# Scan over head pairs: four pairs in sequence against pairs that overlap, with the 32x32 inverses built from 16x16 blocks

## The chip, the cores and the metric

The kernel runs on one core of one Trainium2 chip. The metric is device time in microseconds (us), the median over runs of one program. TensorE is called PE, VectorE DVE, ScalarE ACT, GpSimd POOL; SP issues DMAs.

## The reference, cut to what matters

A two-layer backbone (512 latent and 256 context tokens, width 1024). Each layer mixes the tokens in four ways, merges them with gates and adds an expert network. The change touches the second mixer alone, RWKV-7 time mixing: for each of 8 heads a 64x64 state S runs once forward and once backward over the tokens, the context's state carried into the latent tokens.

```
def step(S, inp):
    r, w, k, v, kk, a = inp
    sa = jnp.einsum('bhij,bhj->bhi', S, kk)
    S = S * w[:, :, None, :] - sa[..., None] * (kk * a)[:, :, None, :] + v[..., None] * k[:, :, None, :]
    return S, jnp.einsum('bhij,bhj->bhi', S, r)
...
o = o_f + o_b
mu = jnp.mean(o, axis=-1, keepdims=True)
var = jnp.mean(jnp.square(o - mu), axis=-1, keepdims=True)
o = (o - mu) * lax.rsqrt(var + RWKV_GN_EPS) * ln_g + ln_b
y = (o + bonus).reshape(B, L, RWKV_W) * f['g']
```

## The kernel before

The scan is done in chunks of 64 tokens: 12 chunks, 4 of context and 8 latent. Heads go in pairs (two heads of 64 fill 128 rows), so a layer has four pairs, and `rwkv_pair` (L690) does one pair for both directions d. Its parts, in the order in which they stand:

- **Gram products** (L709): for each chunk a 128x128 product of the scaled keys BK and queries AR, four chunks and two heads to a group, each group masked out of PSUM by DVE into G (L712). Six groups in a pair.
- **Inverse.** Each chunk needs the inverse of a triangular 64x64 matrix. Its two diagonal 32x32 blocks are copied out of G (L718, ACT), transposed on DVE so that one block lies in one partition (L721, L722), and inverted there by `eliminate` (L735): row by row, a product of two SBUF tiles into `tmp` (L742) and a subtraction from X (L745), 52 of each in a pair, in two column strips that alternate. Transposes bring the result back (L756 to L761), and the off-diagonal block follows by two 32x32 products on PE (L764 to L777). The result is TT.
- **KV** (L732): products of G's first half with the values, copied to SBUF by ACT (L734).
- **Recurrence**, 12 steps (L829). One step: four products with the state S (L836), an addition w0s (DVE, L839), four products with TT (L844), two copies to UV (ACT L846, DVE L847), four products with `nat` (L857), and the new S (L868, DVE) out of PSUM and `sp`, the decayed old S from POOL (L867). One step late come the outputs (L807 and L809: the part from S and the part from G, in turn for each of four places) and their copies into Yn (L818, L820). `nat` is a transposed key chunk with a sign (L182, L792).
- **Finish**: the normalisation of Yn, transposes, bonus and gate (L877 to L903).

The finish of a pair is placed behind the next pair's elimination. A scheduler sets the order on each engine from the code's order and its own costs. It fills TensorE with `gate_lat` (L905): 32 chunks of 24 matmuls with 512 columns that project the latent gates. A chunk's weights are loaded by SP, rounded to wH by ACT (L204), and the remainder wL is made by POOL (L205); ACT takes the result out of PSUM (L911). Each weight tile has two buffers and so has the PSUM tile `pl` of a chunk. Attention (L1156 on) comes after the scan.

## Time and profile before

| | |
|---|---|
| Median of 3 runs | 6446.6 us (6434.26 to 6451.8) |
| The profiled execution's own time | 6431.72 us |
| Its span | 6429.8 us |
| Granted TensorE clock, mean | 0.942 of full |
| PE / DVE / ACT / POOL busy | 90% / 70% / 37% / 34% |

The span is the time from the first to the last instruction of the profiled execution. The scan of layer 0 lies at about 580 to 1110 us, that of layer 1 at about 4110 to 4612 us. A PE that is shown busy may still wait inside of its pipeline, so the prediction reads starts of instructions beside busy time. A float32 matmul stands in the trace as two records and a float32r matmul (the gates) as one.

### The profile page before, as it was taken

How to read it: one execution, taken by the hardware profiler on the slowest of the kernel's cores; microseconds unless marked ns; L12 is line 12 of the kernel's file. 1: busy time of each engine (PE TensorE's matmuls, PEld its weight loads, DVE VectorE, ACT ScalarE, POOL GpSimd, SP SyncE). 2: the span in 40 equal slices, each digit the busy share in tenths (PEclk: the TensorE clock that was granted, in tenths of full speed). 3: DMA queues.
4: the chain of work that ended last, by engine and by line, in shares of the span. 5: the costliest groups of instructions: out<-in, count | busy, mean ns of one | idle time of the engine just before them, and what ended most of it. 6: DMA issues, size and time to landing. Idle time of an engine off the chain costs nothing. (4 is left out here: it accounts for less than half of the span.)

```text
span 6429.8 us, 95669 instructions
## 1 busy us (share of the span) xinstructions
PE 5798.9 (90%) x35605; PEld 4788.5 (74%) x35605; DVE 4503.3 (70%) x9402; ACT 2367.3 (37%) x4585; POOL 2210.1 (34%) x1721
## 2 busy tenths in 40 slices
PE   8898998999898998889899788799899888999998
PEld 5677665678776876777677576666667878999998
DVE  6535555677698847888888774545567798588887
ACT  3223222444436842222222332122345467433333
POOL 1101222000138835566555211132200168444442
PEclk9899997999998999999999899889999999999999
DMA  4456222032435678888899535422221546888896
GB/s 173 160 191 192 81 84 79 18 100 69 137 118 198 237 267 309 307 310 315 315 335 329 184 108 179 132 90 77 77 65 55 157 162 229 298 295 291 295 333 245
DMA packets 532161, 1220.90 MB, mean 190 GB/s; under 512 B 46320, under 2 KB 249200, under 8 KB 524016
## 3 DMA queue, kind: packets, MB, share of 16 engines
q1 hardware_dynamic: 339728, 718.16, 34.1%
q0 software_dynamic: 111168, 406.63, 17.3%
q10 hardware_dynamic: 80800, 90.00, 4.1%
q8 instruction: 281, 4.60, 0.3%
q14 instruction: 184, 1.51, 0.1%
HBM read 1041.41 MB, written 173.21 MB: 189 GB/s over the span
## 5 line engine op out<-in xcount | busy, mean ns | idle before, releaser
L1545 PE MATMUL pu<-HX,wH 128*128 128x512 f32 (+2 forms) x4608 | 1325.5, 371 | 10.0 <-ACT ga L1784 5.6
L1545 PEld LDWEIGHTS pu<-HX,wH 128*128 128x128 f32 x4608 | 854.1, 194 | 114.0 <-ACT ga L1784 7.1
L1545 PE MATMUL pu<-HX,wL 128*128 128x512 f32 (+2 forms) x2304 | 846.8, 368 | 40.5 <-POOL wL L1533 35.8
L1008 POOL DMA_INDIRECT row<-in_peer_u,gix x384 | 489.3, 1274 | 510.0 <-DVE row L1655 275.6
L1008 POOL DMA_INDIRECT row<-in_peer_v,gix x384 | 494.2, 1287 | 450.3 <-DVE accn L1664 222.5
L1637 ACT CAST wH<-row 128x1024 fp32r<-128x1024 f32 x384 | 401.9, 1047 | 618.5 <-DMA row<-in_peer_v 282.3
L1796 PE MATMUL pa<-CL,wH 128*128 128x512 f32 (+1 forms) x1536 | 566.8, 369 | 23.7 <-DVE CL L1776 23.2
L1796 PE MATMUL pa<-CH,wH 128*128 128x512 f32 (+1 forms) x1536 | 564.2, 367 | 22.5 <-ACT CH L1771 22.4
L1655 DVE SCALAR_TENSOR_TENSOR row<-row,hn 128x1024 f32<-128x1024 f32 x384 | 502.1, 1318 | 95.7 <-DMA row<-in_peer_u,gix 94.6
L1653 DVE TENSOR_TENSOR wL<-row,wH 128x1024 fp32r<-128x1024 f32 x384 | 477.4, 1243 | 126.5 <-ACT wH L1637 126.5
L1796 PE MATMUL pa<-CH,wL 128*128 128x512 f32 (+1 forms) x1536 | 562.6, 366 | 0.0
L1664 DVE SCALAR_TENSOR_TENSOR accn<-row,gcw,accn 128x1024 f32<-128x1024 f32 x381 | 518.4, 1371 | 61.2 <-DMA row<-in_peer_v,gix 60.2
L1545 PEld LDWEIGHTS pu<-HX,wL 128*128 128x128 f32 x2304 | 444.3, 193 | 98.7 <-POOL wL L1533 41.7
L204 ACT CAST wH<-wr 128x1024 fp32r<-128x1024 f32 (+1 forms) x222 | 231.0, 1043 | 572.5 <-PE pl L176 182.2
L176 PE MATMUL pl<-X,wH 128*128 128x512 f32 x1024 | 398.9, 452 | 3.4 <-DVE qk L585 3.0
L205 POOL TENSOR_TENSOR wL<-wr,wH 128x1024 fp32r<-128x1024 f32 x64 | 215.0, 3364 | 542.3 <-ACT wH L204 491.9
L1456 POOL TENSOR_SCALAR B<-cst,T 128x128 f32<-128x128 f32 x330 | 381.6, 1164 | 34.3 <-PE pg L1472 21.6
L980 POOL TENSOR_TENSOR lnst<-lnst,mhalf 128x4 f32<-128x4 f32 (+3 forms) x8 | 9.4, 1180 | 1096.5 <-DVE lnst L979 1096.5
L1796 PEld LDWEIGHTS pa<-CL,wH 128*128 128x128 f32 x1536 | 291.6, 190 | 69.4 <-DVE CL L1776 38.3
L1796 PEld LDWEIGHTS pa<-CH,wH 128*128 128x128 f32 x1536 | 291.8, 190 | 62.3 <-ACT CH L1771 30.4
L205 DVE TENSOR_TENSOR wL<-wr,wH 128x1024 fp32r<-128x1024 f32 (+1 forms) x158 | 191.1, 1212 | 189.9 <-ACT wH L204 189.0
L1796 PEld LDWEIGHTS pa<-CH,wL 128*128 128x128 f32 x1536 | 291.8, 190 | 30.6
(400 smaller groups left out, 13244.3 us busy)
## 6 DMA issues: line engine op xcount, KB each, us to landing
row<-in_peer_v SPq DMA_DIRECT2D x256, 512.0 KB, 5.9
wr<-in_uT SPq DMA_DIRECT2D x128, 512.0 KB, 4.9
row<-in_uT SPq DMA_DIRECT2D x128, 512.0 KB, 5.7
wr<-in_ada_w SPq DMA_DIRECT2D x96, 512.0 KB, 6.6
wr<-in_w_gate SPq DMA_DIRECT2D x96, 512.0 KB, 3.7
gdr<-gall SPq DMA_DIRECT2D x32, 1024.0 KB, 6.4
Gt<-gdr SPq DMA_DIRECT2D x32, 1024.0 KB, 13.0
gdr<-big SPq DMA_DIRECT2D x24, 1024.0 KB, 4.8
```

The lines of the kernel that those rows point to most:

```text
L176: pe.matmul(o, lw, rw[:, lo:hi], start=(k == 0 and a == 0), stop=(k == nk - 1 and a == 2))
L204: ac.copy(H, raw)
L205: lsplit[0] = (split or ve).tensor_tensor(L, raw, H.bitcast(F32), op=OP.subtract)
L980: gp.tensor_tensor(st, st, mhalf.to_broadcast([P, 2 * nb]), op=OP.pow)
L1008: gp.indirect_dma_start(out=rows, out_offset=None, in_=tab, in_offset=bass.IndirectOffsetOnAxis(ap=ix, axis=0))
L1456: (gp if e == "gp" else ve).tensor_scalar(B[:, j, :], iota, T3[:, 1, t_ + j:t_ + j + 1], T3[:, 2, t_ + j:t_ + j + 1], op0=OP.is_equal, op1 ...
L1545: pe.matmul(pw[:, :hi - lo], w[:, k, :], x[:, k, :], start=(k == 0 and i == 0), stop=(k == DC - 1 and i == 2))
L1637: ac.copy(H, ready[nx[1]])
L1653: ve.tensor_tensor(L, raw, H.bitcast(F32), op=OP.subtract)
L1655: ve.scalar_tensor_tensor(raw, raw, 1.0, hn[y], op0=OP.mult, op1=OP.mult, accum_out=acts[y][:, j:j + 1])
L1664: ve.scalar_tensor_tensor(accn[y], raw, gcw[y][:, j:j + 1], accn[y], op0=OP.mult, op1=OP.add)
L1796: pe.matmul(pv[:, :TD], w[:, ds], x, start=(k == 0 and i == 0 and (fresh or s == 0)), stop=(k == 1 and i == 2 and (fresh or s == NS - 1)))
```

## The change

The pair's work is split into four generators: `gram` (Gram products and KV), `inverse`, `recurrence` and `finish`. `together` interleaves them: behind the steps of pair hp's recurrence stand the finish of pair hp-1, the inverse of pair hp+1 and the Gram products of pair hp+2. Operands are no longer loaded as half sequences but in pieces: four chunks for a Gram group, three for KV, one step (both directions) for the recurrence; that is 424 more DMAs on SP. G is split into GA (for KV and the inverse) and GR (for the outputs), each with its own mask instruction.

The inverse eliminates inside of 16x16 blocks, both blocks of a 32x32 matrix in one instruction: 15 products and 15 subtractions in a pair in place of 52 and 52. Two transposes of all 128 partitions take the result back, and the rest is done on PE: three more rounds of 32x32 products (Zp, XT, the diagonal blocks of TT), then the two rounds that were there. In all five rounds neighbouring matmuls lie in different quadrants of the array.

In the recurrence the four S parts of an output stand first and then the four GR parts; TT's products and S's share one PSUM tile `pa`. PSUM is divided anew: one tile `pp` for all of `gram` and `inverse`, one `pa`, one `py`, and one `pl` for the gates where there were two.

```diff
-                psc = e2.enter_context(tp(name=f"s2c{l}", bufs=2, space=PSUM))
-                psl = e2.enter_context(tp(name=f"s2l{l}", bufs=2, space=PSUM))
-                psw = e2.enter_context(tp(name=f"s2w{l}", bufs=1, space=PSUM))
...
+                psr = e2.enter_context(tp(name=f"s2r{l}", bufs=1, space=PSUM))
+                psg = e2.enter_context(tp(name=f"s2g{l}", bufs=1, space=PSUM))
+                psl = e2.enter_context(tp(name=f"s2l{l}", bufs=1, space=PSUM))
...
+                def gram(hp, st):
...
+                    def quad(d, q):
+                        aq, bq = [rv.tile([P, 4, P], F32, name=nm(n), tag=n, bufs=2) for n in ("aq", "bq")]
...
+                        pg = wide("pp")
...
+                        ve.tensor_tensor(GA[d][:, :, q * 4:q * 4 + 4, :], p4[:, :, :, 0:64],
...
+                        ve.tensor_tensor(st.GR[d][q], p4[:, :, :, 64:128],
...
-                    cols = [eliminate(SPLIT, 32), eliminate(0, SPLIT)]
...
+                    for u in range(15, 0, -1):
+                        n = 16 - u
...
+                        ve.tensor_tensor(tv, blocks(W, 0, u, u, u + 1).to_broadcast([P, 2, u, n]),
+                                         blocks(X, u, u + 1, u, 16).to_broadcast([P, 2, u, n]), op=OP.mult)
+                        xs = blocks(X, 0, u, u, 16)
+                        ve.tensor_tensor(xs, xs, tv, op=OP.subtract)
+                        yield
...
+                    ve.transpose(Ta.rearrange("p n r -> p r n"), X)
+                    ve.transpose(Tb.rearrange("p n r -> p r n"), X.rearrange("p s t -> p t s"))
...
+                    quads = [(d, q, d * 64 + q * 32) for q in range(2) for d in range(2)]
+                    pz = wide("pp")
                     for p in range(NP):
+                        for d, q, p0 in quads:
+                            pe.matmul(pz[p0:p0 + 32, p * 32:p * 32 + 32], Bm[p0:p0 + 32, p, :], T0T[d][p0:p0 + 32, p, :],
+                                      start=True, stop=True)
...
+                        if S is not None:
+                            for d, h, c, o in outs:
+                                pe.matmul(o, AR[h * 64:h * 64 + 64, d, 64:128],
+                                          S[h * 64:h * 64 + 64, d, :], start=True, stop=False)
+                        for d, h, c, o in outs:
+                            pe.matmul(o, st.GR[d][c // 4][:, h, c % 4, :], UV[:, d, h * 64:h * 64 + 64],
+                                      start=(S is None), stop=True)
...
+                def together(main, others):
...
+                    for s, _ in enumerate(main):
+                        for o in others:
+                            for _ in range(o[2]):
+                                if s >= o[0]:
+                                    o[0] = next(o[1], 0) or 0
...
                 for hp in range(4):
-                    pair = rwkv_pair(hp, nxt, pair)
-                    nxt = next(pair)
+                    others = []
+                    if hp:
+                        others.append([0, finish(hp - 1, st[hp - 1]), 1])
+                    if hp < 3:
+                        others.append([0, inverse(hp + 1, st[hp + 1]), 2])
+                    if hp < 2:
+                        others.append([4, gram(hp + 2, st[hp + 2]), 1])
+                    together(recurrence(hp, st[hp]), others)
```

Outside of the two scans the order on every engine stays as it was, but that in layer 1 attention's first work is mixed into the scan's end. Three places show what moved.

On DVE, in an inverse. Before (first pair of layer 0), L742 and L745 stand alone:

```order
L745 TENSOR_TENSOR X_4734<-X_4734,tmp_4908 128x14x8
L742 TENSOR_TENSOR tmp_4912<-W_4803,X_4734 128x207
L742 TENSOR_TENSOR tmp_4914<-W_4803,X_4734 128x117
L745 TENSOR_TENSOR X_4734<-X_4734,tmp_4912 128x23x9
L745 TENSOR_TENSOR X_4734<-X_4734,tmp_4914 128x13x9
```

Now (second pair of layer 0; L762 and L765 are the product and the subtraction; UV, S, Yn and w0s belong to the first pair's recurrence; GA and GR are the masks of a third pair's Gram group):

```order
L762 TENSOR_TENSOR tmp_5755<-W_5541,X_5538 128x128
L925 SCALAR_TENSOR_TENSOR S_5675<-pa,pcs,sp_5676 128x64
L925 SCALAR_TENSOR_TENSOR S_5675<-pa,pcs,sp_5679 128x64
L876 TENSOR_TENSOR Yn_5476<-Yn_5476,py 64x128 x2
L765 TENSOR_TENSOR X_5538<-X_5538,tmp_5755 128x2x8x8
L901 TENSOR_TENSOR w0s_5717<-pa,KV_4838 128x128
L762 TENSOR_TENSOR tmp_5758<-W_5541,X_5538 128x126
L689 TENSOR_TENSOR GA_5761<-pp,cst 128x2x256
L908 COPY UV_5601<-pa 64x128
L765 TENSOR_TENSOR X_5538<-X_5538,tmp_5758 128x2x7x9
L693 TENSOR_TENSOR GR_5777<-pp,cst 128x512
```

The elimination now stands between the instructions of another pair's step, one or two at a time.

On PE, from one group of S products to the next group of TT products. Before (L176 are gates, pl):

```order
L836 MATMUL pw_5323<-S_5316,AR_4705 64x64 x2
L836 MATMUL pw_5323<-S_5316,AR_4710 64x64 x2
L807 MATMUL pw_5338<-S_5273,AR_4705 64x64
L809 MATMUL pw_5338<-UV_4713,G_4737 64x64
L807 MATMUL pw_5338<-S_5273,AR_4705 64x64
L809 MATMUL pw_5338<-UV_4713,G_4737 64x64
L807 MATMUL pw_5338<-S_5273,AR_4710 64x64
L809 MATMUL pw_5338<-UV_4716,G_4738 64x64
L807 MATMUL pw_5338<-S_5273,AR_4710 64x64
L809 MATMUL pw_5338<-UV_4716,G_4738 64x64
L844 MATMUL pc<-w0s_5328,TT 64x64 x4
```

Now (L898 S products, L862 and L865 the two parts of the output, L905 TT, L685 a Gram product of another pair, L179 gates):

```order
L685 MATMUL pp<-aq_5763,bq_5764 128x128 x3
L898 MATMUL pa<-S_5675,AR_5599 64x64 x4
L685 MATMUL pp<-aq_5763,bq_5764 128x128
L862 MATMUL py<-S_5675,AR_5599 64x64 x4
L185 MATMUL pt<-cst,BK_5819 128x128
L905 MATMUL pa<-w0s_5717,TT_4940 64x64 x4
L185 MATMUL pt<-cst,BK_5819 128x128
L179 MATMUL pl<-X_113,wH_9605 128x512
L179 MATMUL pl<-X_112,wL_9606 128x512
L865 MATMUL py<-UV_5601,GR_4753 64x64
L179 MATMUL pl<-X_112,wH_9605 128x512
L914 MATMUL pa<-UV_5601,nat_5587 64x64 x4
```

The two parts of the output no longer alternate, and other pairs' products stand where gates stood.

On ACT, after the last recurrence of layer 0. Before, no gate is left there; now 326 of the 768 gate matmuls stand behind the last output on PE (314 in layer 1), and ACT has for each chunk:

```order
L207 CAST wH_10115<-wr_10113 128x1024
L982 ACTIVATE glat_10076<-pl 128x512
L983 DMA gscr<-glat_10076 128x512
L207 CAST wH_10149<-wr_10147 128x1024
L982 ACTIVATE glat_10110<-pl 128x512
L983 DMA gscr<-glat_10110 128x512
```

The rounding of the chunk after next (L207) stands ahead of the instruction that empties `pl` (L982); names rise by 34 from chunk to chunk.

## Rows read from the trace of the kernel before

**Rows 1.** The page: busy us, share of the span, instructions of an engine.

```profile
...
PE 5798.9 (90%) x35605; PEld 4788.5 (74%) x35605; DVE 4503.3 (70%) x9402; ACT 2367.3 (37%) x4585; POOL 2210.1 (34%) x1721
```

**Rows 2.** Busy time by stretch, scan of layer 0; columns in its first line.

```profile
...
core 0: us, PE busy (x) PEld busy (x) DVE busy (x) ACT busy (x) POOL busy (x), PEclk, DMA share, GB/s
579.30:644.20 64.90, 54.17 (x516) 43.13 (x515) 52.36 (x119) 16.46 (x25) 24.11 (x8) 0.86 0.46 150
644.20:702.60 58.40, 58.40 (x533) 39.08 (x532) 14.94 (x55) 16.63 (x49) 15.57 (x23) 0.98 0.29 89
...
899.20:955.80 56.60, 56.46 (x532) 37.63 (x531) 16.12 (x56) 16.73 (x51) 16.55 (x25) 1.00 0.20 64
...
1091.00:1109.80 18.80, 2.72 (x9) 1.92 (x9) 7.04 (x10) 3.87 (x5) 3.54 (x3) 0.50 0.55 187
sum 530.50, PE 466.92 PEld 340.02 DVE 294.38 ACT 138.93 POOL 152.01; mean PE 51.88 PEld 37.78 DVE 32.71 ACT 15.44 POOL 16.89
```

**Rows 3.** Busy time by stretch, scan of layer 1.

```profile
...
4179.10:4235.10 56.00, 56.00 (x481) 36.47 (x480) 13.40 (x51) 15.62 (x45) 15.61 (x23) 0.94 0.31 92
...
sum 501.60, PE 446.87 PEld 323.48 DVE 286.04 ACT 132.00 POOL 148.39; mean PE 49.65 PEld 35.94 DVE 31.78 ACT 14.67 POOL 16.49
```

**Rows 4.** Timeline of one step: start, us, engine, line, operands.

```profile
...
674.17 0.34 PE L836 MATMUL pw<-S,AR 64*64 64x64 f32 x8
...
674.35 0.28 PE L807 MATMUL pw<-S,AR 64*64 64x64 f32 x2
...
676.36 0.46 PE L844 MATMUL pc<-w0s,TT 64*64 64x64 f32 x8
...
677.63 0.45 PE L857 MATMUL pw<-UV,nat 128*64 128x64 f32 x8
...
678.20 0.48 DVE L868 SCALAR_TENSOR_TENSOR S<-pw,pcs,sp 128x64 f32<-128x64 f32 x2 [1.01 <-PE pw L857]
...
678.59 0.85 POOL L867 TENSOR_SCALAR sp<-S,pcs 128x64 f32<-128x64 f32 x2 [1.81 <-DVE S L868]
...
679.13 0.34 PE L836 MATMUL pw<-S,AR 64*64 64x64 f32 x8
```

**Rows 5.** Groups by line and shape, scan of layer 0: busy us, mean ns.

```profile
...
L204 ACT CAST wH<-wr 128x1024 fp32r<-128x1024 f32 x32 | 33.5, 1048 | 121.0 <-PE pl L176 99.0 <-issue 10.5 <-DMA AR<-arscr 5.8
L761 DVE STREAM_TRANSPOSE TT<-X 32x1024 f32<-32x1024 f32 x16 | 33.1, 2071 | 0.5
L709 PE MATMUL pw<-AR,BK 64*128 64x128 f32 x384 | 29.5, 297 | 6.6 <-issue 3.5 <-DVE G L712 1.7 <-DMA AR<-arscr 1.4
...
L911 ACT ACTIVATE glat<-pl 128x512 f32<-128x512 f32 x32 | 18.9, 592 | 2.0 <-PE pl L176 2.0
...
L732 PE MATMUL pc<-UV,G 64*64 64x64 f32 x384 | 15.6, 233 | 6.0 <-DVE G L712 4.0 <-ACT KV L734 2.1
...
L780 DVE TENSOR_SCALAR TT<-pw 32x768 f32<-32x768 f32 x4 | 3.9, 963 | 11.1 <-ACT TT L779 11.1
```

**Rows 6.** Timeline of PE, 32x32 products of the off-diagonal block, first pair.

```profile
...
640.14 1.11 PE L774 MATMUL pw<-TT,Z 32*32 32x32 f32 x30
...
641.12 0.19 PE L777 MATMUL pw<-TT,Z 32*32 32x32 f32 x1
641.12 0.19 PE L774 MATMUL pw<-TT,Z 32*32 32x32 f32 x1
```

**Rows 7.** Timeline of PE, KV products of the second pair.

```profile
...
713.55 1.26 PE L732 MATMUL pc<-UV,G 64*64 64x64 f32 x34
```

**Rows 8.** Busy time of the gates' line alone, a stretch full of them.

```profile
...
600.00:605.40 5.40, 5.40 (x24) 4.35 (x25) 1.00 0.44 150
```

**Rows 9.** POOL's line L205 in layer 0: ns min/median/max, first and last start.

```profile
...
L205 POOL TENSOR_TENSOR wL<-wr,wH x30: 2345/2382/11224, 579.6 to 1033.0; 128x1024 fp32r<-128x1024 f32 x30
```

**Rows 10.** DVE's line L742 in layer 0, same columns.

```profile
...
L742 DVE TENSOR_TENSOR tmp<-W,X x208: 170/262/2528, 599.7 to 1007.0; 128x60 f32<-128x60 f32 x8, 128x31 f32<-128x31 f32 x4, 128x87 f32<-128x87 f32 x4, 128x112 f32<-128x112 f32 x4
```

**Rows 11.** Timeline of DVE, the elimination of the first pair.

```profile
...
614.17 4.78 DVE L745 TENSOR_TENSOR X<-X,tmp 128x150 f32<-128x150 f32 x2
```

More of the change, by code (lines that the diff above doesn't have):

```diff
@@ L693, in rwkv_pair, with both, chunks @@
-                def rwkv_pair(hp, loaded, others):
-                    AR, BK, UV = loaded
-                    PCs = [pcs[:, hp, d, :] for d in range(2)]
+                class Pair:
+                    pass
+                def both(hp, i, s):
+                    t = arscr[hp, 0, i]
+                    return bass.AP(tensor=t.tensor, offset=t.offset + fo[s] * P,
+                                   ap=[[NCH * P, P], [2 * P * NCH * P + (bo_[s] - fo[s]) * P, 2], [1, P]])
+                def chunks(hp, a, n):
+                    return vnscr[hp].rearrange("t b two i -> t (b two) i")[:, a:a + n, :]
@@ L748, in rwkv_pair @@
-                    cols = [eliminate(SPLIT, 32), eliminate(0, SPLIT)]
-                    while cols:
-                        for x in list(cols):
-                            if next(x, 0) == 0:
-                                cols.remove(x)
-                    for _ in others:
-                        pass
-                    XT = rv.tile([P, 32, 32], F32, name=nm("XT"), tag="W", bufs=1)
-                    ve.transpose(XT[0:32].rearrange("p n r -> p r n"), X[0:32])
-                    ve.transpose(XT[96:128].rearrange("p n r -> p r n"), X[96:128].rearrange("p s t -> p t s"))
@@ new lines, in inverse @@
+                    XT = ft("XT").rearrange("p (n t) -> p n t", t=32)
+                    for d, q, p0 in (quads[0], quads[3]):
+                        (ve.tensor_copy if d else ac.copy)(XT[p0:p0 + 32],
+                                                           px[p0:p0 + 32, :T].rearrange("p (n t) -> p n t", t=32))
+                    yield
+                    pt32 = wide("pp")
+                    for p in range(NP):
+                        for d, q, p0 in quads:
+                            pe.matmul(pt32[p0:p0 + 32, p * 32:p * 32 + 32], Zp[p0:p0 + 32, p, :], T0[d][p0:p0 + 32, p, :],
+                                      start=True, stop=True)
@@ L781, in rwkv_pair, with recurrence, load @@
+                    ve.tensor_scalar(tt[96:128, :, 0:32], po[96:128, :T].rearrange("p (n t) -> p n t", t=32), -1.0, None,
                                      op0=OP.mult)
-                    following = fetch_pair(hp + 1) if hp < 3 else None
-                    Yn = rw.tile([P, 6, P], F32, name=nm("Yn"), tag="Yn")
-                    S = None
+                    yield
+                def recurrence(hp, st):
+                    PCs = [pcs[:, hp, d, :] for d in range(2)]
+                    tt = st.tt
+                    st.Yn = Yn = rw.tile([P, 6, P], F32, name=nm("Yn"), tag="Yn", bufs=2)
+                    def load(s):
+                        ar = rv.tile([P, 2, P], F32, name=nm("AR"), tag="AR", bufs=4)
+                        sy.dma_start(ar, both(hp, 0, s))
+                        uv = rv.tile([P, 2, P], F32, name=nm("UV"), tag="UV", bufs=4)
+                        sy.dma_start(uv[64:128, 0:1, :], chunks(hp, fo[s], 1))
+                        sy.dma_start(uv[0:64, 1:2, :], chunks(hp, 11 - s, 1))
+                        return ar, uv
```

297 lines of the change are left out of this document (165 added, 132 removed).

## The prediction

> **What bounds the kernel now.** The page comes first: PE is busy for 90% of the span, so at first sight taking DVE's work out of the way should bring little [rows 1]. The view that decides is the busy time by stretch, cut at the first Gram product, at the first product with TT and at the last S of each pair. The scan of layer 0 takes 530.5 us [rows 2], that of layer 1 501.6 [rows 3]. In the preparation of the first pair (64.9 us) DVE is busy for 52.36 us, in its recurrence (58.4 us) for 14.94, while PE is busy in both [rows 2]: the two stretches have different limits and stand one behind the other. What keeps PE busy in a preparation is mostly gates, which are owed by the end of the scan and no earlier.
>
> A recurrence is a chain. The timeline of one step runs from S products at 674.17 to S products at 679.13: 4.96 us. Between them stand TT at 676.36, `nat` at 677.63 and S on DVE at 678.20 [rows 4]. From 674.35 to 676.36 (2.0 us) PE works on the outputs of the step before, L807 and L809 in turn, before it comes to TT, although w0s needs only the S products: here a group of eight small products that isn't on the chain sits in it, because PE takes its work in order. The reader should see that "PE busy" here means busy with the wrong thing.
>
> DVE pays for POOL in the preparation. wL on POOL takes 2.38 us as a rule and up to 11.2 [rows 9]; a product L742 on DVE takes 0.26 as a rule and up to 2.53 [rows 10], and two subtractions together once 4.78 [rows 11]. Each holds up the other when both read two SBUF tiles. The Trainium skill ("SBUF — State Buffer", section "Who interferes with whom") says that a DVE instruction with two SBUF inputs contends with a GpSimd instruction that reads SBUF, by an exclusive lock. The trace agrees: 2.4 us is the length of one wL.
>
> **The sum, for one layer of four pairs.**
>
> *First preparation, nothing to hide behind.* From the first Gram product (579.3 [rows 2]) up to the first elimination instruction (599.7 [rows 10]) nothing gets shorter: 20.4 us. The elimination has 30 instructions at 0.262, 7.9 us, instead of 104, several of them locked. Two transposes at 2.07 [rows 5] are 4.1. Then five rounds on PE; the 32x32 products start 31.7 ns apart in one quadrant ((1.11 - 0.19)/29), and the last of L777 and the first of L774, in different quadrants, start together [rows 6]. 336 matmuls are 672 records: one behind the other 21.3 us, with neighbours overlapped some 1.6 us a round. To each round I add an evacuation of 0.9 (L780, 0.963 [rows 5]) and 0.4 of hand-over: 14.5 for the five. Sum 47; with one lock of 2.4 us, 50, against 64.9.
>
> *Recurrences.* The first and third of layer 0 take 58.4 and 56.6 us [rows 2], the mean of the first three is 57.2. The new order of the outputs puts four products of one kind behind each other, as the groups for S (eight records, 0.34 us) and for `nat` (0.45) are now [rows 4]: 0.56 us for both halves in place of 2.0, 1.4 a step, 16.8 in 12 steps. Against it comes the work that now stands inside of a recurrence, and PE's part of it stands in order before the chain's own products: Gram 29.5/4 = 7.4 us and KV 15.6/4 = 3.9 [rows 5], the five rounds 8. That is 19.3, taken in full: gates between the steps give way, but I can't see that the chain's gaps (about 1.3 us between TT and `nat`, 1.5 from `nat` to S products) take all of it in. For the seam between two recurrences I add 6 us (26 gates stand in the first, 24 take 5.40 us [rows 8]), for DVE locks 4. So 57.2 - 16.8 + 19.3 + 10 = 69.7, three times, and the last without an inverse 44: 253 us. In layer 1, where 481 PE instructions stand in a recurrence of 56.0 us [rows 3] and the outputs are less in the way (I take 8 steps of gain, 11.2): 55.5 - 11.2 + 19.3 + 10 = 73.6, three times, and 44: 265.
>
> *The tail.* Before, no gate is left behind the last recurrence; PE is busy for 2.7 of the last 18.8 us there [rows 2]. Now 326 of 768 gate matmuls stand there, 13.6 chunks of 24. On PE a chunk is 5.4 us plus 0.2. But `pl` is single now: the products of the next chunk wait for ACT's L911, and on ACT the rounding of the chunk after next stands ahead of it. So between two chunks PE waits for ACT's rounding and L911, 1.05 + 0.59 [rows 5] and 0.1 of hand-over: 7.35 us per chunk, **100 us** in layer 0. What is queued behind is the gates alone, and attention behind them. In layer 1 (314, 13.1 chunks, 96 us) attention's first products stand between the chunks and I give 18 us back: 78.
>
> *Edits at nothing.* 424 more SP loads: 76 or so in a pair at an issue of about 0.4 us are 30 of its 66 us on SP, which otherwise loads gate weights; without that room an operand of a step would come late, and rival (2) has that price too. The single `pp` makes a Gram group wait for the mask of the one before, which is behind a step's DVE work: PE does the steps meanwhile. DVE's work for a preparation, with the second mask of each Gram group, is still some 50 us (now 52.36 [rows 2]); a recurrence of 69.7 us, of which its own work takes 14.94 [rows 2], has 55 for it. If that cover were gone, rival (2) shows the price. Copies of TT's parts go to ACT, which is busy for 16.6 of 58.4 us [rows 2].
>
> Layer 0: 50 + 253 + 100 = 403 for 530.5, -127. Layer 1: 50 + 265 + 78 = 393 for 501.6, -108. Together -235; the profiled execution took 6431.7 us, so 6197. The median of the runs shown lies 14.9 above that execution: **6210 us**.
>
> **What isn't known, from both sides.** The overlapped 32x32 rounds: between 1.6 us each, as the pairs that start together [rows 6] bear out, and 4.3 (21.3/5), if one waits for the other; the rounds write one PSUM tile from different row quadrants, and the nearest row is KV, where 34 records in two row halves pass in 1.26 us [rows 7], 37 ns each and not slower than in one. I take 1.6. The tail: between 5.6 us a chunk (rounding early) and 7.35; I take the upper, because the rounding stands ahead of L911 on ACT in every chunk; the lower would give 24 + 23 us. The seams and locks: 0 to 28 us a recurrence.
>
> **Rivals.** (1) *Everything fits beside.* PE's gaps in the chain take in the Gram products and rounds, seams and locks cost little: 40 us less in each layer, some 6130. For it: a step has about 2.8 us in which PE has no work of the chain. Against: PE's order is fixed, and one product that waits for DVE holds up the chain.
>
> (2) *DVE late in each step.* An elimination instruction or a mask from PSUM stands between `nat`'s result and S, and some of them meet a wL: 1.5 us more in each of 36 steps in a layer, 108 for both: 6318. For it: the locks [rows 9 to 11], and in the order an elimination or a mask stands within one or two instructions of S or UV. Against: where S is due, its own instructions stand ahead.
>
> (3) *The quadrants don't overlap.* Then 21.3 - 8 = 13.3 us more in a pair, eight pairs, +106: 6316. The trace speaks against it: starts of different quadrants lie together [rows 6, 7]. The Trainium skill ("TensorEngine Tiling (Array Packing)", section "Restrictions and Gotchas", "Gotcha 1: PSUM Pressure") says that different row tiles cannot access the same PSUM bank simultaneously, and all four quadrants of a round write one tile; by that rule this rival would be the outcome. The KV products [rows 7] show two row halves writing one tile without a gap, so I don't follow it.
>
> (4) *POOL starves: slower than before.* wL takes 11.2 us instead of 2.38 when DVE's eliminations stand close [rows 9], 8.8 each. Now eliminations stand in every step, and `sp` of the chain is POOL's too: if a wL is in front of it and waits for DVE, S waits. To eat the gain of 235 us takes 3.3 us in each of 72 overlapped steps, one starved wL in 2.7 steps; in every second step it would be 36 x 8.8 = 317, some 6530. Against it: a lone elimination of 0.26 us leaves DVE's port free again soon, and only a close row of them held POOL so long.
>
> (5) *Nothing changes.* The gates that gave way come back whole in the tail, and PE was the limit after all: about 6440. Against: PE's products are the same, but the outputs' 1.4 us a step are waits inside of "busy", and DVE's 52 us in a preparation become cover.
>
> **How the numbers follow.** Forecast 0.54, rival (1) 0.15, (2) 0.20, (3) 0.06, (4) 0.03, (5) 0.02. A measurement of this kernel can tell about 0.3% (19 us) from no change. Faster holds the forecast and rivals 1 to 3, short of two that come together: 0.94; slower holds (4) and such a heap: 0.04; same (5): 0.02. The forecast's own range is 6150 to 6270; the bounds of (1) to (3) widen the range to 6100 and 6340.
>
> **What would show it.** The scan (first Gram product to attention's first product) should take about 403 and 393 us. A step of the first pair's recurrence should take 5.5 to 6 us with an output group of 0.6 us, and 3.6 without other work (last pair). In the rounds, records of different quadrants should start within 10 ns. In the tail the last products of a chunk and the first of the next should lie about 2 us apart, with ACT's rounding between. A wL of over 5 us, or an idle time of DVE before S that ends with `sp`, would speak for (4); gates at 5.6 us a chunk for (1). The forecast is wrong if the steps' length with all other work exceeds 7 us, or if the scan's end doesn't move while its recurrences do.

## The result and the profile after

The changed kernel takes **6355.25 us** (median of 4 runs, 6346.6 to 6366.0) where the kernel before took 6440.43 beside it: a ratio of 0.9858 with a 95% interval from 0.9833 to 0.9882, 85 us faster. Forecast were 6210 us and a range of 6100 to 6340. The direction was right; of the gain a good third came. The profiled execution took 6350.55 us, its span is 6348.5.

The page after, answering to [rows 1], with the group of gate products on PE:

```profile
...
PE 5717.3 (90%) x39445; PEld 4730.2 (75%) x39445; DVE 4331.5 (68%) x8864; ACT 2394.2 (38%) x4617; POOL 2177.3 (34%) x1745
...
L179 PE MATMUL pl<-X,wH 128*128 128x512 f32 x1024 | 381.5, 441 | 35.9 <-ACT glat L982 35.9
...
```

PE's share is still 90%. New is the idle time of 35.9 us before gate products, which ends with `glat` on ACT.

Busy time by stretch of the changed kernel, layer 0 (answers to [rows 2], columns as there). The rows are: first preparation; first recurrence, and the stretch from its last TT to the second pair's first; the same for the second and the third pair; fourth recurrence; tail up to attention's first product.

```profile
...
582.90:652.90 70.00, 55.59 (x986) 41.89 (x985) 32.07 (x52) 19.41 (x31) 13.46 (x9) 0.88 0.49 147
652.90:728.80 75.90, 67.84 (x1254) 50.10 (x1254) 43.59 (x110) 26.30 (x64) 18.98 (x26) 0.96 0.51 151
728.80:742.10 13.30, 12.48 (x252) 9.53 (x247) 9.57 (x13) 4.24 (x6) 5.37 (x4) 1.00 0.53 160
742.10:818.90 76.80, 66.88 (x1180) 47.69 (x1179) 41.27 (x105) 25.72 (x63) 17.90 (x26) 0.84 0.40 117
818.90:832.40 13.50, 12.40 (x251) 9.48 (x247) 9.79 (x13) 4.24 (x6) 5.36 (x4) 1.00 0.52 159
832.40:903.20 70.80, 63.20 (x1235) 45.11 (x1234) 41.12 (x101) 27.90 (x66) 19.28 (x25) 0.93 0.30 87
903.20:908.30 5.10, 5.10 (x128) 3.54 (x123) 1.67 (x5) 1.06 (x2) 0.00 (x0) 1.00 0.62 176
908.30:975.00 66.70, 59.65 (x554) 36.94 (x554) 23.19 (x65) 16.49 (x47) 19.57 (x25) 0.80 0.28 84
975.00:1090.30 115.30, 85.55 (x339) 63.80 (x340) 12.29 (x13) 25.01 (x35) 31.82 (x15) 0.95 0.42 138
sum 507.40, PE 428.68 PEld 308.07 DVE 214.55 ACT 150.37 POOL 131.75; mean PE 47.63 PEld 34.23 DVE 23.84 ACT 16.71 POOL 14.64
...
```

The scan takes 507.4 us in place of 530.5, where 403 were forecast. The first preparation (70.0 us) is no shorter than before, a recurrence with another pair's work beside it takes 70.8 to 76.8, and behind each stands a seam of 13.3, 13.5 or 5.1 us. The tail is 115.3. Layer 1 in the same view, its last recurrence and its tail, in which attention already works (its first recurrence takes 78.9 us):

```profile
...
4398.40:4451.30 52.90, 49.31 (x497) 30.50 (x496) 19.12 (x61) 15.41 (x44) 17.83 (x25) 0.94 0.45 143
4451.30:4551.30 100.00, 96.83 (x415) 72.25 (x415) 14.89 (x30) 31.08 (x48) 33.35 (x18) 1.00 0.36 114
...
```

Where a step goes now is told by the timeline of a slow step, first pair of layer 0 (start, length, engine, line, operands, releaser):

```profile
...
672.20 0.34 PE L898 MATMUL pa<-S,AR 64*64 64x64 f32 x8
672.32 0.69 DVE L689 TENSOR_TENSOR GA<-pp,cst 128x512 f32<-128x512 f32 x1 [1.21 <-PE pp L685]
...
672.92 0.68 DVE L693 TENSOR_TENSOR GR<-pp,cst 128x512 f32<-128x512 f32 x1
...
673.52 0.28 DVE L901 TENSOR_TENSOR w0s<-pa,KV 128x128 f32<-128x128 f32 x1
...
673.71 1.16 PE L685 MATMUL pp<-aq,bq 64*128 64x128 f32 x16
...
674.80 0.45 PE L905 MATMUL pa<-w0s,TT 64*64 64x64 f32 x8
...
677.44 1.67 ACT L728 COPY ND<-GA 32x768 f32<-32x768 f32 x2 [1.38 <-DVE GA L689]
...
679.86 0.48 ACT L714 COPY KV<-pp 128x384 f32<-128x384 f32 x1
...
680.24 0.26 ACT L907 COPY UV<-pa 64x128 f32<-64x128 f32 x1
...
681.83 0.45 PE L914 MATMUL pa<-UV,nat 128*64 128x64 f32 x8 [0.31 <-DVE UV L908]
...
```

The S products are done at 672.54, but w0s (L901) stands on DVE behind the two masks of another pair's Gram group (GA, GR) and starts at 673.52. TT then stands on PE behind the next Gram group (L685) and starts at 674.80. The copy UV (L907) stands on ACT behind `glat` (L982, 675.48), the copies ND, which wait for GA, and KV, and starts at 680.24, five microseconds after its input. `nat` (L914) starts at 681.83. These three waits are not for the chain's own data: they are places in line.

Worked out from the records of PE and DVE, for the second to the eleventh step of each recurrence of layer 0: the time between the end of one link of the chain (S products, w0s, TT, UV on DVE, `nat`, S) and the start of the next, summed over a step.

| waits in a step, us | pair 1 | 2 | 3 | 4 |
|---|---|---|---|---|
| before | 2.7 | 2.6 | 2.6 | 2.6 |
| changed | 3.9 | 3.9 | 3.6 | 3.2 |
| changed, pairs one behind the other (run e4) | 1.9 | 2.0 | 2.2 | 1.8 |
| before, outputs in the new order (run e5) | 1.3 | 1.4 | 1.5 | 1.5 |

Link by link, in the first three pairs, the wait grew most ahead of UV, from 0.1 to between 0.7 and 1.2 us; ahead of w0s it grew by 0.3 to 0.5, ahead of `nat` by 0.1 to 0.6, ahead of S by 0.2 at most. Ahead of the S products and of TT it shrank or stayed.

### The profile page after: what moved, and what is told of

It reads as the page before. It is cut to its first block, busy times and chain, and to the rows that moved or that the text cites. A ratio compares the mean times of both kernels' runs of the same rounds, so it can differ in the third digit from the quotient of the medians.

```text
span 6348.5 us, 103908 instructions
## 1 busy us (share of the span) xinstructions
PE 5717.3 (90%) x39445; PEld 4730.2 (75%) x39445; DVE 4331.5 (68%) x8864; ACT 2394.2 (38%) x4617; POOL 2177.3 (34%) x1745
## 5 line engine op out<-in xcount | busy, mean ns | idle before, releaser
L207 ACT CAST wH<-wr 128x1024 fp32r<-128x1024 f32 (+1 forms) x222 | 230.8, 1042 | 570.5 <-PE pl L179 198.6
L179 PE MATMUL pl<-X,wH 128*128 128x512 f32 x1024 | 381.5, 441 | 35.9 <-ACT glat L982 35.9
L208 POOL TENSOR_TENSOR wL<-wr,wH 128x1024 fp32r<-128x1024 f32 x64 | 152.5, 2383 | 582.9 <-ACT wH L207 563.7
L1865 ACT CAST CH<-ga 128x512 fp32r<-128x512 f32 (+1 forms) x256 | 145.2, 567 | 463.9 <-DVE ga L1862 369.5
```

The lines of the kernel that those rows point to most:

```text
L179: pe.matmul(o, lw, rw[:, lo:hi], start=(k == 0 and a == 0), stop=(k == nk - 1 and a == 2))
L207: ac.copy(H, raw)
L208: lsplit[0] = (split or ve).tensor_tensor(L, raw, H.bitcast(F32), op=OP.subtract)
L1865: ac.copy(CC[i][0], at)
```

## The experiments

Two theories stood after this look. **Theory G**: the gates that still stand in the recurrences (66, 45, 58 and 70 matmuls in layer 0), with their rounding and emptying on ACT, stretch the steps. **Theory W**: the other pairs' own work does, by its place in line. Later a third came up, **theory O**: the order of the outputs is the whole gain. Medians and ratios are to runs of the kernel before in the same group of runs.

| run | edit | us | ratio to before (95%) |
|---|---|---|---|
| changed | | 6355 | 0.9858 (0.9833 to 0.9882) |
| e1 | changed, no gates | 6164, one run | |
| e2 | before, no gates | 6373, one run | |
| e3 | UV in two tiles | 6354 | 0.9846 (0.9803 to 0.9889) |
| e4 | pairs one behind the other | 6357 | 0.9854 (0.9813 to 0.9895) |
| e5 | before, outputs in the new order | 6328 | 0.9819 (0.9802 to 0.9837) |
| e6 | inverse earlier | 6351 | 0.9863 (0.9846 to 0.9880) |
| e7 | second PSUM tile in the tail | 6329 | 0.9828 (0.9810 to 0.9846) |
| e8 | e4 with that tile | 6346 | 0.9843 (0.9820 to 0.9865) |
| e9 | changed, outputs in the old order | 6444 | 0.9982 (0.9961 to 1.0003) |
| e10 | e6 and e7 together | 6315 | 0.9773 (0.9734 to 0.9812) |
| e11 | e5, no gates | 6262, one run | |
| e12 | e4, no gates | 6293, one run | |
| e13 | gates written between the steps | 6292 | 0.9772 (0.9740 to 0.9804) |
| e14 | e13 and e6 together | 6285 | 0.9763 (0.9730 to 0.9796) |

### Without gates: the changed kernel and the kernel before

```diff
-                for f in range(32):
-                    gate_lat(f)
+                g = rw.tile([P, TL], F32, name=nm("glat"), tag="glat", bufs=1)
+                gp.memset(g, 0.0)
+                for f in range(32):
+                    sy.dma_start(gscr[f][:, :TL], g)
```

> The changed kernel without the 32 chunks of gate_lat (the gates are left out, zeros stand in their place). Theory G (gates between a step's products, and their rounding and emptying on ACT, stretch the chain): the four recurrences of layer 0, now 322 us from the first TT to the last output, shrink by the 298 gate matmuls that stand in them, 69 us, and by some 20 us of waits for ACT: about 235; with a first preparation of about 55 and 20 at the end the scan is some 310 us, and the whole kernel about 390 us shorter than with gates, 5960. Rival W (the other pairs' work in the order of PE, DVE and ACT stretches it): the recurrences stay above 290 us, the scan about 380, the kernel about 6100.

> The kernel before without gate_lat in the same way. Its recurrences should fall from 57 to about 44 us each (steps of 3.6), the preparations stay at 65 to 70: scan some 470 us against 530.5, the kernel 6320. If the preparations too get shorter (no wL on POOL against the eliminations on DVE), 60 each: 435 us, 6250.

Measured: 6164 and 6373. In the changed kernel the four recurrences with their seams take 292 us in layer 0 (from 646.5 to 938.7) where they took 322 with gates: theory W, most of the stretching is there without a gate. The granted clock is lower in this run, 0.63 to 0.78 in the four recurrences for 0.80 to 0.96 with gates, so the 30 us may understate what the gates cost; run e13 below puts 241 gates more into this stretch and lengthens it by 32 us, about as much. The scan is 383 us. The kernel before went another way than both expectations: its recurrence got longer, 62.8 us in place of 58.4. Two rows say why (first preparation and first recurrence of layer 0, kernel before without gates):

```profile
...
579.50:634.20 54.70, 24.36 (x386) 22.61 (x386) 45.47 (x120) 7.53 (x12) 1.11 (x2) 0.59 0.71 246
634.20:697.00 62.80, 56.91 (x462) 40.18 (x462) 15.39 (x55) 12.84 (x45) 8.59 (x20) 0.50 0.14 45
...
```

The granted clock is 0.50 in the recurrence, the lower of the two levels, where it was 0.98 with gates [rows 2]. In the preparation ahead of it PE is busy for 24.4 of 54.7 us, with gates for 54.2 of 64.9 [rows 2]. So kernels without gates are compared with each other only, and with an eye on their clocks. Without gates the change is worth 209 us, with them 85: something in the gates takes the rest.

### The two copies of UV

```diff
-                        uv = rv.tile([P, 2, P], F32, name=nm("UV"), tag="UV", bufs=4)
+                        uv = [rv.tile([P, 1, P], F32, name=nm("UV"), tag=f"UV{d}", bufs=4) for d in range(2)]
```

> The changed kernel with UV in two tiles, one for each direction, as it was before the change. Theory U: in one tile DVE's copy waits for ACT's (32 us of idle DVE in layer 0), 0.27 us and more in each of 96 steps: 26 to 50 us faster, 6305 to 6330. Rival: other waits take its place in most steps: less than 10 us.

A wait that the change added and the prediction had not seen. The changed kernel's copy of UV on DVE (L908; ns min, median, max, first and last start, then what its idle time before ended with, in us and times):

```profile
...
L908 DVE COPY UV<-pa x47: 278/295/296, 656.9 to 969.2; 64x128 f32<-64x128 f32 x47
...
  ACT UV L907: 32.2, 30
...
```

In the kernel before, all but one of its copies were released by PE. Now 30 of 47 wait for ACT. Measured: 6354, the same as the changed kernel. But the run does not price the wait, for its own trace still has it. The same line of the same view in e3:

```profile
...
  ACT UV L907: 30.2, 31
...
```

So the one tile for UV is not what makes DVE's copy wait. What both copies still share in e3 is the PSUM tile `pa` that they read; the kernel before had a tile `pc` for each direction, and DVE's copy started 0.06 us behind ACT's (median). That `pa` is the cause was not tried, and what the wait costs stays open.

### The overlap undone

```diff
-                    others = []
...
-                    together(recurrence(hp, st[hp]), others)
+                    for _ in gram(hp, st[hp]):
+                        pass
+                    together(inverse(hp, st[hp]), [[0, finish(hp - 1, st[hp - 1]), 1]] if hp else [])
+                    together(recurrence(hp, st[hp]), [])
```

> The changed kernel with its pairs one behind the other (gram, inverse, recurrence of one pair, then the next; finish beside the next inverse): only the overlap is undone. If the overlap is what gains, as forecast: four preparations of about 62 and four recurrences of about 52 and a tail of some 80 make 536 us a layer, 28 more than the changed kernel's 508: about 6410 to 6440. If the new inverse and the order of the outputs gain and the overlap gives back what it hides: 6340 to 6370, the same as the changed kernel.

Measured: 6357, the same as the changed kernel. The overlap gives back all that it hides. It is not undone whole: the scheduler still sets the 96 Gram records of the next pair into each of the first three recurrences, so the run tells of the inverse, the finish and most of KV. Busy time by stretch of this run, layer 0: first recurrence, second preparation, fourth recurrence, tail behind the last TT.

```profile
...
652.90:700.60 47.70, 46.88 (x633) 33.38 (x633) 24.55 (x68) 18.46 (x52) 10.93 (x21) 1.00 0.55 153
700.60:749.30 48.70, 41.28 (x854) 31.14 (x845) 26.87 (x50) 14.96 (x22) 16.20 (x10) 0.89 0.37 110
...
951.80:998.60 46.80, 45.65 (x529) 28.89 (x528) 15.02 (x55) 14.65 (x43) 14.18 (x24) 1.00 0.28 86
998.60:1071.30 72.70, 57.16 (x240) 42.88 (x236) 10.30 (x12) 15.12 (x22) 21.81 (x11) 0.95 0.46 155
...
```

A recurrence takes 47.7 us and the preparation behind it 48.7 (70.4 in the kernel before); both together 96.4, against 89.2 for a recurrence with its seam in the changed kernel. So 48.7 us of hidden work come back as 41.5 us of longer steps and seam. A part of that is the granted clock, 1.00 in this run's recurrences and 0.84 to 0.96 in the first three of the changed kernel; it was not separated. And the stretch that was hidden was not idle: it held 86 gate matmuls (250 in the three preparations between recurrences), which the overlapped kernel puts behind the last output. Behind the last TT stand 216 gates here, in 72.7 us, and 330 in the changed kernel. What is gained in the chain, 26 us in layer 0 (392.1 from the first Gram product to the last output, 417.6 here), is lost in the tail (115.3 from there to attention's first product, 78.6 here).

### The order of the outputs alone

In the kernel before, the products with S and those with G in two loops in place of one:

```diff
                                     pe.matmul(o, AR[d](c)[h * 64:h * 64 + 64, 64:128],
                                               S[h * 64:h * 64 + 64, d, :], start=True, stop=False)
+                        for d in range(2):
+                            for h in range(2):
...
                                 pe.matmul(o, G[d][:, h, c, 64:128], UV[d](c)[:, h * 64:h * 64 + 64],
```

> The kernel before with one edit: the four S parts of an output stand first, then its four G parts, as in the change. As forecast (the group of eight takes 2.0 us alternating and 0.56 in a row, and stands in the chain): steps of 4.9 become 3.5 to 4, about 12 us less in each of 8 recurrences: 6340 to 6360. Rival: the 2.0 us are mostly a wait that the next product would have had anyway (or gates come to stand there): less than 20 us, 6425 or more.

Measured: 6328 us, 113 less than before in the same group, more than was expected and at least as much as the whole change. One step in the timeline of this run (L807 and L814 are the two parts of the output, L841 the S products, L849 TT):

```profile
...
673.12 0.34 PE L807 MATMUL pw<-S,AR 64*64 64x64 f32 x8
...
673.29 0.32 PE L841 MATMUL pw<-S,AR 64*64 64x64 f32 x8
...
673.54 0.46 PE L814 MATMUL pw<-UV,G 128*64 128x64 f32 x8
...
674.36 0.45 PE L849 MATMUL pc<-w0s,TT 64*64 64x64 f32 x8
...
```

The S products and the output's two halves pass in 0.8 us together (673.12 to 673.93) where they took 2.2 with the halves alternating (674.17 to 676.36) [rows 4]. The first recurrence of layer 0 and the sum of the scan:

```profile
...
646.10:692.90 46.80, 46.80 (x532) 31.11 (x531) 14.45 (x55) 16.68 (x49) 14.68 (x23) 0.91 0.32 95
...
sum 486.70, PE 416.98 PEld 305.93 DVE 295.72 ACT 138.82 POOL 155.83; mean PE 46.33 PEld 33.99 DVE 32.86 ACT 15.43 POOL 17.31
...
```

The first recurrence takes 46.8 us for 58.4, the third 47.6 for 56.6 [rows 2], the scan 486.7 for 530.5. From the first TT to the last, the eight recurrences are together 86 us shorter in the traces, and the two profiled executions lie 85 apart (6346.66, the slowest of e5's four, for 6431.72). S parts use 64 rows of the array and G parts 128 (64*64 and 128*64 in the rows). The Trainium skill ("TensorEngine Tiling (Array Packing)", section "Tiling Modes", "Key Properties") says that a change of the tiling mode, not of the tile alone, drains TensorE; the trace agrees: alternating, the group costs 1.4 us more, with eight changes of shape for two. A rival is that a G part waits because it adds to the place that the S part just ahead of it wrote. The step of before speaks against it (timeline of PE, kernel before):

```profile
...
674.56 0.33 PE L809 MATMUL pw<-UV,G 128*64 128x64 f32 x2
...
674.82 0.33 PE L807 MATMUL pw<-S,AR 64*64 64x64 f32 x2
...
675.07 0.33 PE L809 MATMUL pw<-UV,G 128*64 128x64 f32 x2
...
```

From a G part to the next S part, which writes another place, it is 0.26 us, from an S part to its G part 0.25. So the price goes with the change of shape, some 0.23 us each (an estimate: 1.4 us for six changes). That a drain is what takes the time was not tried by itself.

The new inverse has the fate of the overlap. Against e5, run e4, which has it one pair behind the other, is 48 us faster from layer 0's first Gram product to its last output (417.6 for 465.9), and its tail, to attention's first product, is 58 us longer (78.6 for 20.8).

The opposite edit in the changed kernel, the old order put back:

```diff
-                        if S is not None:
-                            for d, h, c, o in outs:
+                        for d, h, c, o in sorted(outs, key=lambda x: x[:2]):
+                            if S is not None:
...
-                        for d, h, c, o in outs:
```

> The changed kernel with the two parts of an output in turn again, as before the change; all else of the change stays. Theory O (the order of the outputs is the whole gain, the overlap and the new inverse gain nothing in the sum): 85 to 113 us slower than the changed kernel, 6440 to 6470, no faster than before. Rival: beside the other pairs' work the wait of an alternating output is hidden in part: 6380 to 6400.

Measured: 6444, a ratio of 0.9982 whose interval takes in 1. Theory O holds for the sum: without the new order of the outputs the change gains nothing that can be measured.

### The seam and the tail

Inverse at three pieces a step, finish from the fifth step on:

```diff
-                        others.append([0, finish(hp - 1, st[hp - 1]), 1])
+                        others.append([4, finish(hp - 1, st[hp - 1]), 1])
...
-                        others.append([0, inverse(hp + 1, st[hp + 1]), 2])
+                        others.append([0, inverse(hp + 1, st[hp + 1]), 3])
```

> The changed kernel with the inverse of the next pair at three pieces a step in place of two, and the finish of the pair before from the fifth step on. Theory S (the 13.4 us between two recurrences are the last rounds of an inverse that came too late): the seams shrink to 5 us or less and the recurrences keep their length: 20 to 48 us faster, 6307 to 6335. Rival C (work of another pair costs the same wherever it is put): seams shrink, recurrences grow by as much: 6345 to 6365.

Measured: 6351. The seams of layer 0 fall to 2 us each, 26 less in all, but its first recurrence grows from 76.0 to 89.6 and the first three by 22: rival C. From the first Gram product to the last output layer 0 gains 12 us in the trace, which is of the fastest execution (6331); the median gains 4, within its uncertainty.

The tail of the changed kernel in its timeline, between two chunks:

```profile
...
1066.95 0.39 PE L179 MATMUL pl<-X,wL 128*128 128x512 f32 x1
1067.19 1.04 ACT L207 CAST wH<-wr 128x1024 fp32r<-128x1024 f32 x1 [5.76 <-PE pl L179]
1068.14 0.59 ACT L982 ACTIVATE glat<-pl 128x512 f32<-128x512 f32 x1
...
1068.78 0.73 PE L179 MATMUL pl<-X,wH 128*128 128x512 f32 x2 [1.44 <-ACT glat L982]
...
```

PE's last product of a chunk starts at 1066.95, ACT rounds the chunk after next (L207), then empties `pl` (L982), and PE goes on at 1068.78: a chunk takes 7.30 us, 7.35 were forecast. With a second tile:

```diff
-                    pw = psl.tile([P, 512], F32, name="pl")
+                    pw = wide("pp") if f >= 19 and f % 2 else psl.tile([P, 512], F32, name="pl")
```

> The changed kernel with every second gate chunk from the 19th on in the PSUM tile pp, which is free by then. If PE's pause between two chunks of the tail (1.44 us idle, 7.30 us a chunk) is the single pl, a chunk takes 5.6 to 5.8 us there: 13.7 chunks x 1.6 = 22 us in layer 0 and up to 18 in layer 1: 6315 to 6333. Rival: the weights come no faster (ACT's rounding, POOL's remainder): less than 10 us.

> The sequential kernel (pairs one behind the other, as in the run before) with the same second PSUM tile for gates, from the 23rd chunk on. It has 9 chunks of the tail and not 13.7, so it gains less: 10 to 25 us, 6333 to 6347. If the overlap pays only by what it moves to the tail, the overlapped kernel with two tiles is 10 to 20 us ahead of this one; if not, they are equal again.

Measured: 6329 and 6346, both in their ranges; the 17 us between the two are not clear of noise, since their intervals overlap. In the first of the two, PE goes from tile to tile without a pause, one chunk in 5.60 us:

```profile
...
1035.86 0.63 PE L179 MATMUL pl<-X,wH 128*128 128x512 f32 x2
...
1041.46 0.63 PE L179 MATMUL pp<-X,wH 128*128 128x512 f32 x2
...
```

> The changed kernel with both edits that took something away: the inverse at three pieces a step (no seam) and the second PSUM tile for the gates of the tail. If they add, 26 + 4 to 17 us under the changed kernel: 6312 to 6325, ahead of the kernel before with the new order of the outputs alone (6328). If the seam's work only moves: 6329.

Measured: 6315, 41 us under the changed kernel, where the two edits alone gave 4 and 26.

### What the gates cost the overlap

> The kernel before with the new order of the outputs and without gates (they are left out). Without gates the kernel before took 6373 and the changed one 6164. If the order of the outputs is worth the same here, 12 to 20 us in each of 8 recurrences: 6215 to 6275, and the overlap with the new inverse is worth the rest, 50 to 110 us, which the gates then eat. If the order is worth little without gates: 6350, and all of the 209 us are overlap and inverse.

> The sequential kernel without gates (they are left out). If the overlap hides what it was forecast to hide, three preparations a layer of some 45 us, it is 200 us or more behind the overlapped kernel without gates (6164): 6360 or more. If a pair's work costs nearly as much beside a recurrence as behind it: 6180 to 6230.

Measured: 6262 and 6293. Without gates the order of the outputs is worth 111 us, as much as with them (113), and the overlap 129 (e12 to e1) where it is worth 2 with them. This lies between the two expectations for e12: six preparations of 48.9 us (one of e12's, taken for all: an estimate) would be 293, so less than half is hidden. And a part of the 129 is clock. The first recurrence of e12, layer 0:

```profile
...
652.50:717.90 65.40, 63.01 (x606) 46.85 (x608) 24.95 (x69) 17.94 (x52) 8.80 (x21) 0.50 0.35 98
...
```

At a granted clock of 0.50 it takes 65.4 us, where it takes 47.7 with gates at 1.00 (e4); the overlapped kernel's stands at 0.78 without gates. How much of the 129 this makes was not separated. Left open was whether PE has room for the gates inside of the recurrences.

```diff
+                chunk = iter(range(32))
+
+                def gates(n):
+                    for s in range(n):
+                        if s % 2:
+                            gate_lat(next(chunk))
+                        yield
...
-                    others = []
+                    others = [[0, gates(13), 1]]
...
-                for f in range(32):
+                for f in chunk:
                     gate_lat(f)
```

> The changed kernel with the same gates written between the steps, one chunk in every second step, so that 72 of 768 gate matmuls stand behind the last output in place of 326 (691 instead of some 300 inside). Theory R (PE has free time inside of the overlapped recurrences, and the tail is only the order's fault): the recurrences grow by less than 0.1 us for each gate moved, the tail of layer 0 falls from 115 to about 35: 60 to 110 us faster, 6245 to 6295. Rival F (a gate costs its 0.23 us and more wherever it stands, since it stands in line with the chain's products): 254 gates lengthen the recurrences of layer 0 by 58 us or more and shorten the tail by 77: 6320 to 6360, and slower than the changed kernel if ACT's rounding and emptying of chunks hold up UV too.

> The same with the inverse at three pieces a step and the finish from the fifth step on, so no seam. By theory R another 5 to 20 us less than the run before, 6235 to 6285; by rival F 6310 to 6350, no better than the version with a second PSUM tile in the tail (6315).

Measured: 6292, 64 us under the changed kernel, in theory R's range, if at its end; with the earlier inverse 6285, not clear of the run before. Last recurrence of layer 0 and its tail in e13:

```profile
...
940.10:1005.80 65.70, 63.04 (x629) 43.86 (x628) 21.57 (x64) 22.51 (x59) 23.58 (x28) 1.00 0.44 135
1005.80:1044.00 38.20, 23.53 (x85) 17.09 (x86) 12.69 (x13) 8.94 (x15) 7.97 (x5) 0.84 0.60 201
...
```

The tail is 38.2 us for 115.3, and from the first Gram product to the last output it takes 423.7 for 392.1. Behind the last TT stand 89 gates for 330. So 241 gates fewer in the tail save 0.32 us each and cost 0.13 each in the chain: of a gate's 0.23 us a little less than half is hidden beside the chain. That is between theory R, which asked for less than 0.1, and rival F. **e14 is the fastest version here**, by the medians 43 us ahead of e5, and 166 ahead of the kernel before in its group.

## Why the prediction was wrong, step by step

**What bounds it.** Right in its core: the group of output products is not on the chain, sits in it, and was the place to look. It was priced at 1.4 us a step, which is what the group itself loses in e5; a recurrence was to lose 16.8 us (layer 0) and 11.2 (layer 1), and e5 shows 8.8 to 12.2 and 6.5 to 13.7. This term alone, measured, is the whole result.

**The first preparation**, 50 forecast, 70.0 measured. "Nothing gets shorter" up to the elimination was wrong the other way: it starts 26.4 us behind the first Gram product, not 20.4. The six Gram groups pass one by one through the single `pp`, each with two masks of 0.68, and through two buffers of operands that now come in pieces; two of the six wait on PE for such a load. The loads had been set at nothing. One of the two (changed kernel, timeline of PE):

```profile
...
590.51 1.16 PE L685 MATMUL pp<-aq,bq 64*128 64x128 f32 x16 [1.71 <-DMA aq<-arscr]
...
```

The elimination took 12.6 with two instructions of 2.1 and 2.3 us, each while a wL runs on POOL (7.9 and one such lock of 2.4 were forecast). The five rounds took 27 us and not 14.5. I priced one evacuation of 0.9 for a round, but ACT and DVE each take a half out of one PSUM tile into one tile, and DVE's half starts when ACT's is done (changed kernel, timeline of DVE in the first preparation):

```profile
...
642.13 1.92 DVE L803 COPY TT<-pp 32x768 f32<-32x768 f32 x2 [7.58 <-ACT TT L803]
...
```

The evacuation of TT alone takes 4.9 us (639.13 to 644.05), with the rounding of a gate chunk between ACT's two copies. Besides, the third round stops for 2.1 us (last section), and the fourth starts 2.0 us after TT, behind gates on PE. The products themselves were priced well: 1.6 us a round, 1.7 to 1.8 in four of five in e4.

**Recurrences with work beside them**, 69.7 forecast, 89.2, 90.3 and 75.9 measured with their seams in layer 0, 91.5, 81.9 and 69.9 in layer 1. This is the largest miss, 46 us of layer 0's 104. I took 19.3 us for PE's share of the hidden work and 10 for seam and locks; against run e4 the hidden work costs 41.5, 41 and 25 us. The step that failed is "Edits at nothing": DVE's work was said to be covered and ACT's copies to find room. They have room in the sum (DVE 43.59 us busy in the first recurrence's 75.9), but not in line: w0s waits behind masks on DVE, TT behind a Gram group on PE, UV behind copies on ACT. Waiting is 1.0 to 1.3 us a step more than before and 1.4 to 2.0 more than in e4; over eleven steps that is some three quarters of the 20 to 28 us by which these recurrences are longer than e4's. The other part of the 41.5 is the seam, 13.3 where 6 were forecast. Rival (2), DVE late by 1.5 us a step, comes nearest in size, but it put the wait ahead of S, and there it grew by 0.2 us at most; it grew ahead of UV, w0s and `nat`.

**The last recurrence**, 44 forecast, 66.7 and 52.9 measured. The 70 gates in it are not the reason: e4's last recurrence of layer 0 has as many and takes 46.8 us. What the changed kernel adds is the finish of the third pair, which the 44 did not price (changed kernel, DVE and PE):

```profile
...
918.60 3.08 DVE L958 TENSOR_TENSOR Yn<-Yn,gvar 128x768 f32<-128x768 f32 x1 [2.41 <-POOL gvar L956]
...
922.25 0.34 PE L862 MATMUL py<-S,AR 64*64 64x64 f32 x1 [4.96 <-DVE S L925]
...
```

This instruction takes 0.96 us in the other pairs of layer 0; here a wL on POOL started 0.07 us ahead of it (918.53). S stands behind it on DVE, and PE has nothing for 4.96 us. The granted clock is then 0.50 for most of 10 us, and after a second pause (1.67 us, up to 946.07) for most of 17 more; over this recurrence it is 0.80, and 1.00 in e4's. What pause and clock each cost was not separated.

**The tail**, 100 forecast, 115.3 measured, of which 107 are gates and 8.3 the way from the last gate to attention, which I had forgotten. The period of a chunk was right to 0.05 us. The four misses of layer 0, 20, 46, 23 and 15, are its 104 us. In layer 1 the first preparation took 66.9 us, the three recurrences 243.3 for 221 and the last 52.9: 48 us more in all. Its tail took 100.0 for 78, but attention's first work is in it, and what follows the scan is 20 us shorter than before (1797 for 1817 us), so this term was right to 2 us. Layer 0's 104 and these 50 are the 154 us by which the profiled execution missed 6197.

**The rivals.** (1) fell. (3) fell: rows of different quadrants start within 10 ns of each other while they write one tile (below). (4) fell: wL on POOL has no long execution any more (changed kernel, ns min, median, max):

```profile
...
L208 POOL TENSOR_TENSOR wL<-wr,wH x18: 2337/2372/2388, 580.9 to 968.6; 128x1024 fp32r<-128x1024 f32 x18
...
```

2388 ns at most, where it was 11224 [rows 9]: an elimination spread between other instructions did not hold POOL. (5), that the gates "come back whole in the tail", is nearer to what happened to the overlap than its chance of 0.02: what the overlap gained, the gates gave back; only the outputs' gain stayed.

## What to carry to other kernels

Ask what the engines did in a stretch before hiding it: if a filler ran there, the filler has to go somewhere, and it is paid at the price of its new place (here 0.32 us a gate in a tail with one PSUM tile, 0.13 between the steps). Work hidden beside a chain costs by its place in each engine's line, not by its share of busy time, so price it from the links of the chain. And try each part of a large change alone first: one loop written as two is all of the gain that was measured, and the rest, hidden work and moved gates, came to nothing in the sum.

## What was not expected of the hardware

**Dense short products stall on nothing visible.** In the third round (96 matmuls of 32x32 in four quadrants, 192 records) PE stops in the middle, for 2.3 us in the first inverse of the changed kernel and for 2.2 to 2.6 in three of the eight of e4. Changed kernel, timeline of PE behind such a stop:

```profile
...
638.59 0.18 PE L800 MATMUL pp<-Ta,Zp 32*32 32x32 f32 x1 [2.11 <-issue]
638.60 0.21 PE L800 MATMUL pp<-Tb,Zp 32*32 32x32 f32 x1
638.60 0.21 PE L800 MATMUL pp<-Ta,Zp 32*32 32x32 f32 x1
638.61 0.21 PE L800 MATMUL pp<-Tb,Zp 32*32 32x32 f32 x1
...
```

"issue" is time for which the profile names no releaser. From 634 to 640 us the only DMA is of the instruction queue, two packets, and none of it falls into the stop. The cause stays open. The rows also show the four quadrants: four records start within 20 ns into the same columns of one tile `pp`. The Trainium skill ("TensorEngine Tiling (Array Packing)", section "Restrictions and Gotchas", "Gotcha 1: PSUM Pressure") says that different row tiles cannot access one PSUM bank simultaneously; here they overlap, 192 records in 1.82 us (second pair of e4), 9.5 ns a record against 31.7 in one quadrant. The measurement decides.

**Less work, slower steps.** Leaving the gates out of the kernel before lengthened its first recurrence from 58.4 to 62.8 us, with the granted clock at 0.50 in place of 0.98, though the whole kernel got faster (6373 for 6449). Run e13 shows it the other way round: its last recurrence of layer 0 holds 143 gates up to the last output where the changed kernel's holds 76, and takes 65.7 us for 66.7, at a granted clock of 1.00 for 0.80. In these two stretches the filler on PE paid for itself.
